# A hybrid S5 / RG-LRU / attention block: a fourth buffer of split weights, splits three units ahead, and the S5 tables as a task of their own

## The chip, the cores and the metric

The kernel runs on one core of one Trainium2 chip. The metric is device time in microseconds (us), the median of several runs. Engines are named as the profile names them: PE multiplies matrices (PEld is its weight load), ACT evaluates functions and copies, DVE does elementwise arithmetic, POOL is a second, slower elementwise engine, SP issues most DMAs.

## The reference

One layer, sequence 256, width 2048, everything in float32. Three branches run side by side on the same normed input, each is multiplied by a sigmoid gate, and a squared-ReLU MLP follows.

```python
xn = rms_norm(x)
u_s5, u_lru, q, k, v, gate_logits = split(xn @ w_in)       # 1024 x 5, then 3 x 2048
g_s5, g_lru, g_attn = split(sigmoid(gate_logits + b_gate))
# S5: 64 groups of 16 channels, 64 complex states each, diagonal linear scan over time
a = exp(lam * dt); h = linear_scan(a, B u); y = Re(C h) + d * u
y_s5 = gelu(y) * sigmoid(gelu(y) @ w_glu + b_glu)
# RG-LRU: causal conv of 4, two block-diagonal sigmoid gates, real linear scan
y_lru = linear_scan(exp(log_a), sqrt(1 - exp(2 log_a)) * (i * xc))
# stick-breaking attention, 8 heads of 128
w = exp(log_sigmoid(z) + reverse_cumsum(log_sigmoid(-z)))   # causal
merged = g_s5 * (y_s5 @ w_br_s5) + g_lru * (y_lru @ w_br_lru) + g_attn * (y_attn @ w_br_attn)
h = x + merged @ w_out
out = rms_norm(h + relu(rms_norm(h) @ w_up)**2 @ w_down)
```

## The kernel before

**Weights.** All weights pass once through the core as 520 units, each 256 rows by 512 columns of one matrix, 512 KB. The order is written in `stream`: w_in for the LRU (units 0 to 15) and for S5 (16 to 31); the LRU gate, four times eight units of w_in and four of w_br_lru (32 to 79); k, q, v twice (80 to 127); the attention gate, four times eight and four (128 to 175); two chunks of S5 gates (176 to 191); w_glu (192 to 199); the rest of the S5 gates with w_br_s5; w_out; w_up and w_down in turns.

**Splits.** A float32 product is done as three products of rounded parts. A unit is loaded by SP into a `raw` buffer (pool `wraw`, three buffers). `split_next` makes `hi`, the rounded copy, on ACT (line 146) and `lo = raw - hi` on DVE (line 147), in pool `whi`, three buffers of each. PE then does 12 matmuls of 512 columns for the unit (`chunk_tok`, lines 241 to 243; `pair_tok`, lines 276 to 278) or 24 of 256 columns (`chunk`, lines 225 to 227): hi by xhi, lo by xhi and hi by xlo. `next_unit(i)` issues loads up to unit i + 3 and splits up to unit i + 2 ahead of the products of unit i.

**Side tasks.** Everything else is written as Python generators. `later` puts one in a list with a rate; after the products of each unit `pump` steps each task by its rate, and what a step issues stands between the instructions of that unit. A scheduler then settles the order on each engine, and an engine executes its own instructions in that order.

**The S5 task.** `s5_scan` runs at rate `S5_RATE`, 1.27, from unit 32 on, over eight blocks of eight groups. For each block it needs a table of cosines and sines of the phases of its states over time (`tc`, `ts`, 128 x 1024). `s5_tables(b)` adds two small tables by broadcast (`fhi`, `flo`, two POOL products of 512 columns made once for all blocks), takes the fraction of a turn (line 606 on ACT, one DVE row), an Abs (line 609) and two Sin (lines 610 and 611). Its generator `more` is stepped by three `next(more, None)` inside the block before: the parts stand at fixed places of that block. A block multiplies by the table, scans over time, multiplies back and ends in the matmuls `ps_y`. After the last block come gelu (Square, Tanh) and `yg_hi`, `yg_lo`, the operands of w_glu.

**Gates and functions.** After a gate chunk the two banks are scaled and biased on DVE (line 750) and go through a Sigmoid on ACT (line 751). Sigmoid, Sin and the exponentials lie in different function tables, and ACT_TABLE_LOAD changes the table.

The functions that the change touches:

Of the kernel before, what the change touches and what calls it, by code (L numbers as in the profile page):

```python
# [14 lines left out]
P = 128  # L15
L = 256
# [30 lines left out]
def hybrid_block(ctx: ExitStack, tc: tile.TileContext, io, out):  # L47
# [61 lines left out]
    raw, hi, anchor = {}, {}, {}  # L109
    st = {"load": 0, "split": 0, "use": 0}  # L110

# [96 lines left out]
    def finish(task):  # L208
        while step(task):
            pass  # L210
# [21 lines left out]
    def chunk_tok(name, c, k, xs, hold=0, done=None):  # L232
# [77 lines left out]
    ux = sp.tile([P, 4, L], F32R, name="ux")  # L310
    stk = sp.tile([96, NT, 2, L], F32R, name="stk")
    rad = sp.tile([P, 32], F32, name="rad")
    fhi = sp.tile([P, 32, 16], F32, name="fhi")
    flo = sp.tile([P, 32, 16], F32, name="flo")
    pp = s5.enter_context(tc.tile_pool(name="s5w", bufs=1))
# [96 lines left out]
    def s5_params():  # L412
# [14 lines left out]
        g.tensor_scalar(b, b, math.pi, -math.pi, ALU.min, ALU.max)  # L427
        yield
        g.tensor_scalar(w, b, 1.0 / TWO_PI, None, ALU.mult)
# [3 lines left out]
        g.tensor_tensor(n, cr, n, ALU.subtract)  # L433
        sb = steps.unsqueeze(1).broadcast_to([P, 32, 16])
        g.tensor_tensor(flo, w.unsqueeze(2).broadcast_to([P, 32, 16]), sb, ALU.mult)
        g.tensor_tensor(fhi, n.unsqueeze(2).broadcast_to([P, 32, 16]), sb, ALU.mult)
        yield
# [56 lines left out]
    nc.gpsimd.memset(tiny, 2.0 ** -115)  # L494
    wr = lp.tile([P, WT, P], F32, name="wr")
    wi = lp.tile([P, WT, P], F32, name="wi")
    for t, src in ((wr, "lru_w_r"), (wi, "lru_w_i")):
# [97 lines left out]
    def s5_tables(b):  # L595
        c = pp.tile([P, NT, 16, 16], F32, tag="tc", name=f"tc{b}", bufs=2)
        s = pp.tile([P, NT, 16, 16], F32, tag="ts", name=f"ts{b}", bufs=2)
        q = slice(b * NT, (b + 1) * NT)
        sh = [P, NT, 16, 16]
        f = "p n a b -> p (n a b)"  # L600
        cf, sf = c.rearrange(f), s.rearrange(f)

        def gen():
            nc.vector.tensor_tensor(c, fhi[:, q, :].unsqueeze(3).broadcast_to(sh), flo[:, q, :].unsqueeze(2).broadcast_to(sh), ALU.add)
# [4 lines left out]
            nc.scalar.activation(cf, sf, AF.Abs)  # L609
            nc.scalar.activation(sf, sf, AF.Sin, scale=-TURN)  # L610
            nc.scalar.activation(cf, cf, AF.Sin, scale=-TURN, bias=half_pi)
            yield
        f = "p n a b -> p n (a b)"
        return (c.rearrange(f), s.rearrange(f)), gen()

    def s5_split(ct):
# [3 lines left out]
        for g in range(2):  # L620
            m = mask[:, g:g + 1]
            nc.scalar.activation(bx[0][:, :, g, :], bco[:, ct], AF.Copy, scale=m)
            nc.vector.scalar_tensor_tensor(bx[1][:, :, g, :], bco[:, ct], m, bx[0][:, :, g, :].bitcast(F32), ALU.mult, ALU.subtract)

    def s5_stack(t):
        for i, w_ in enumerate((ux[:, 0:4:2, :], ux[:, 1:3, :], ux[:, 0:4:3, :])):
            nc.sync.dma_start(stk[i * 32:i * 32 + 32, t].bitcast(F32), w_[t * 32:t * 32 + 32].bitcast(F32))
# [3 lines left out]
    def s5_scan():  # L631
# [11 lines left out]
        tt = nc.vector.tensor_tensor  # L643
        for b in range(WT):
            c, s = tabs
            t3 = pp.tile([P, NT, L], F32, tag="t3", name=f"t3_{b}")
            for t in range(NT):
# [22 lines left out]
            tt(t3, t3, vr, ALU.subtract)  # L670
            next(more, None)
            yield
            for x_ in (t1, t3):
                for t in range(NT):
# [4 lines left out]
                    yield  # L679
            next(more, None)  # L680
            tt(t2, t1, c, ALU.mult)
            yield
            tt(vr, t3, s, ALU.mult)
            next(more, None)
            yield
# [15 lines left out]
            if b % 2:  # L701
                gq.append(later([gelu(b)], 1.0))

    def tt_scan(o, r, i):
        nc.vector.tensor_tensor_scan(o, r, i, 0.0, ALU.mult, ALU.add)

    def gelu(b):
        y = us5[:, b - 1:b + 1, :]
        g1 = tmp.tile([P, 2, L], F32, tag="gate", name=f"g1_{b}", bufs=3)
        nc.scalar.activation(g1, y, AF.Square)  # L710
        nc.vector.scalar_tensor_tensor(g1, g1, 1.0 / GELU_K, y, ALU.add, ALU.mult)
        yield
        nc.scalar.activation(g1, g1, AF.Tanh, scale=GELU_C * GELU_K)
        nc.vector.scalar_tensor_tensor(y, g1, 1.0, y, ALU.add, ALU.mult)
        yield
# [19 lines left out]
    def gates(idx, c, alloc):  # L735
# [49 lines left out]
    def attention(hs, kT, qT, vt):  # L785
# [49 lines left out]
    for c in range(2):  # L835
# [10 lines left out]
        banks = chunk_tok("w_in", 8 + c, D, xs)  # L846
        vt = ap_.tile([P, 2, CH], F32, tag="v", name=f"vt{c}")
        for t in range(2):
# [73 lines left out]
    gp = small("norm_mlp_g")  # L922
    x_tok = mlp.tile([P, 2, D], F32, name="xres")

# [75 lines left out]
    gfb = mlp.tile([P, D], F32, name="gfb")  # L1000
    ho = mlp.tile([P, 2, D], F32, name="ho")
    ssq = mlp.tile([P, 2, 6], F32, name="ssq")
# [168 lines left out]
```

## Time and profile before

| | us |
|---|---|
| median of 3 runs | 1511.09 (1510.91 to 1512.21) |
| the profiled execution | 1512.1 |
| its span, first to last instruction | 1510.3 |
| PE busy | 1488.4 |
| DVE busy | 1175.2 |
| ACT busy | 782.3 |
| POOL busy | 35.3 |

The mean granted clock of PE is 0.995. In the rows of single engines the first number is the start from the beginning of the span, the second the duration, and what stands in brackets is the idle time before it with the work that ended it. Matmuls overlap, so a matmul's duration is longer than the distance to the next start, and a busy PE is not PE at its peak. In a table of stretches a value such as "7.82 (x51)" is busy time and count of instructions in that stretch.

### The profile page before, as it was taken

Reading aid. Unit: us, or ns where it says so; the run is one execution under the profiler, and the core shown is the slowest. Engines: PE = TensorE matmul, PEld = TensorE weight load, DVE = VectorE, ACT = ScalarE, POOL = GpSimd, SP = SyncE. Lnnn points to the kernel's source line nnn. Section 1 sums busy time; section 2 is a strip of 40 time slices with the busy share of each in tenths; the row PEclk is TensorE's granted clock in tenths of the full one; section 3 lists DMA queues with packets and bytes.
Section 4 is the critical chain, followed back from the end, with each engine's and each line's share of the span. In section 5 each row is a group of like instructions: output and inputs, shape, how many; then the busy total and the mean of one; then the engine's idle time right before and its main releaser. Section 6 shows DMA issues by size and latency. Waiting matters only on the chain.

```text
span 1510.3 us, 19900 instructions
## 1 busy us (share of the span) xinstructions
PE 1488.4 (99%) x7518; PEld 1260.5 (83%) x7518; DVE 1175.2 (78%) x1468; ACT 782.3 (52%) x920; POOL 35.3 (2%) x60
## 2 busy tenths in 40 slices
PE   9999999999999999999999999999999999999997
PEld 9997788989887878988887888888888888888886
DVE  6767998897988989689799796568854787558965
ACT  6767556565765564544455544344433444344443
POOL 1400000000000000000000000000000000000011
PEclk9999999999999999999999999999999999999999
DMA  9546766665555666666855666666666666666664
GB/s 287 157 153 176 228 205 201 187 182 168 175 172 183 208 182 210 189 202 190 276 182 188 197 184 205 194 185 196 198 194 193 193 195 195 195 191 191 192 197 152
DMA packets 89858, 292.41 MB, mean 194 GB/s; under 512 B 12834, under 2 KB 17058, under 8 KB 89634
## 3 DMA queue, kind: packets, MB, share of 16 engines
q1 hardware_dynamic: 89618, 291.07, 62.6%
q8 instruction: 59, 0.97, 0.3%
q14 instruction: 37, 0.30, 0.1%
q10 hardware_dynamic: 144, 0.07, 0.0%
HBM read 282.71 MB, written 2.10 MB: 189 GB/s over the span
## 4 chain that ended last, share of the span: by engine, by line
PE 83%; DVE 9%; issue 3%; ACT 2%; DMA 2%; SPq 0%; DVEq 0%; ACTq 0%
PE mt_w_up L242 6%; PE mt_w_up L241 6%; PE mt_w_up L243 6%; PE mt_w_in L242 5%; PE mt_w_in L243 5%; PE mt_w_in L241 5%; PE mt_w_down L242 4%; PE mt_w_down L241 4%; PE mt_w_down L243 4%; PE mp_w_down L277 4%; PE mp_w_down L278 4%; PE mp_w_down L276 4%; PE mm_w_in L227 4%; PE mm_w_in L225 4%; PE mm_w_in L226 4%; DVE lo L147 3%
## 5 line engine op out<-in xcount | busy, mean ns | idle before, releaser
L146 ACT CAST hi<-raw 128x1024 fp32r<-128x1024 f32 (+1 forms) x521 | 545.2, 1049 | 625.9 <-PE mt_w_up L243 131.4
L147 DVE TENSOR_TENSOR lo<-raw,hi 128x1024 fp32r<-128x1024 f32 (+1 forms) x521 | 637.9, 1225 | 287.7 <-ACT hi L146 284.1
L242 PE MATMUL mt_w_in<-lo,xhi 128*128 128x512 f32 x448 | 176.1, 393 | 3.9 <-DVE lo L147 3.7
L241 PE MATMUL mt_w_in<-hi,xhi 128*128 128x512 f32 x448 | 175.2, 396 | 0.2 <-ACT hi L146 0.2
L243 PE MATMUL mt_w_in<-hi,xlo 128*128 128x512 f32 x448 | 175.2, 391 | 0.0
L241 PE MATMUL mt_w_up<-hi,hhi 128*128 128x512 f32 x448 | 174.3, 389 | 0.0
L242 PE MATMUL mt_w_up<-lo,hhi 128*128 128x512 f32 x448 | 174.3, 389 | 0.0
L243 PE MATMUL mt_w_up<-hi,hlo 128*128 128x512 f32 x448 | 174.3, 389 | 0.0
L227 PE MATMUL mm_w_in<-xhi,lo 128*128 128x256 f32 x512 | 145.4, 286 | 4.5 <-DVE lo L147 4.5
L225 PE MATMUL mm_w_in<-xhi,hi 128*128 128x256 f32 x512 | 146.5, 286 | 0.5 <-ACT hi L146 0.4
L226 PE MATMUL mm_w_in<-xlo,hi 128*128 128x256 f32 x512 | 145.7, 285 | 0.0
L728 DVE STREAM_TRANSPOSE reluT<-relu 32x256 f32<-32x256 f32 x256 | 111.5, 436 | 4.2
L242 PEld LDWEIGHTS mt_w_in<-lo,xhi 128*128 128x128 f32 x448 | 84.6, 189 | 24.0 <-DVE lo L147 7.6
L227 PEld LDWEIGHTS mm_w_in<-xhi,lo 128*128 128x128 f32 x512 | 98.7, 194 | 5.5 <-DVE lo L147 5.5
L242 PE MATMUL mt_w_down<-lo,hd_hi 128*128 128x512 f32 (+1 forms) x272 | 102.5, 377 | 0.0
L241 PE MATMUL mt_w_down<-hi,hd_hi 128*128 128x512 f32 (+1 forms) x272 | 102.4, 377 | 0.0
L243 PE MATMUL mt_w_down<-hi,hd_lo 128*128 128x512 f32 (+1 forms) x272 | 102.4, 376 | 0.0
L225 PEld LDWEIGHTS mm_w_in<-xhi,hi 128*128 128x128 f32 x512 | 99.2, 194 | 1.1 <-ACT hi L146 1.0
L277 PE MATMUL mp_w_down<-lo,hd_hi 128*128 128x512 f32 x256 | 99.8, 390 | 0.1
L278 PE MATMUL mp_w_down<-hi,hd_lo 128*128 128x512 f32 x256 | 99.6, 389 | 0.0
L276 PE MATMUL mp_w_down<-hi,hd_hi 128*128 128x512 f32 x256 | 99.6, 389 | 0.0
L241 PEld LDWEIGHTS mt_w_in<-hi,xhi 128*128 128x128 f32 x448 | 84.5, 189 | 17.8 <-ACT hi L146 0.7
(299 smaller groups left out, 2370.2 us busy)
## 6 DMA issues: line engine op xcount, KB each, us to landing
raw<-in_w_in SPq DMA_DIRECT2D x175, 512.0 KB, 4.3
raw<-in_w_up SPq DMA_DIRECT2D x128, 512.0 KB, 4.2
raw<-in_w_down SPq DMA_DIRECT2D x128, 512.0 KB, 4.2
raw<-in_w_out SPq DMA_DIRECT2D x32, 512.0 KB, 4.2
raw<-in_w_br_lru SPq DMA_DIRECT2D x16, 512.0 KB, 4.6
raw<-in_w_br_attn SPq DMA_DIRECT2D x16, 512.0 KB, 4.1
raw<-in_w_br_s SPq DMA_DIRECT2D x16, 512.0 KB, 4.1
stk<-ux SPq DMA_DIRECT2D x96, 64.0 KB, 4.1
```

The lines of the kernel that those rows point to most:

```text
L146: anchor["act"] = nc.scalar.copy(h[:, k, :], r[:, k, :]).ins
L147: anchor["dve"] = nc.vector.tensor_tensor(l_[:, k, :], r[:, k, :], h[:, k, :].bitcast(F32), ALU.subtract).ins
L225: nc.tensor.matmul(o, wh[:, kk, s], xh, start=first and ct % 2 == 0, stop=False, skip_group_check=True)
L226: nc.tensor.matmul(o, wh[:, kk, s], xl, start=False, stop=False, skip_group_check=True)
L227: mm = nc.tensor.matmul(o, wl[:, kk, s], xh, start=False, stop=last and ct % 2 == 1, skip_group_check=True)
L241: nc.tensor.matmul(banks[j], xh[:, s], wh[:, a:b], start=kt == 0, stop=False)
L242: nc.tensor.matmul(banks[j], xh[:, s], wl[:, a:b], start=False, stop=False)
L243: return nc.tensor.matmul(banks[j], xl[:, s], wh[:, a:b], start=False, stop=kt == ng * UK - 1)
L276: nc.tensor.matmul(o, xh[:, s], wh[:, kk, :], start=kt == 0, stop=False)
L277: nc.tensor.matmul(o, xh[:, s], wl[:, kk, :], start=False, stop=False)
L278: mm = nc.tensor.matmul(o, xl[:, s], wh[:, kk, :], start=False, stop=kt == ng * UK - 1)
L728: nc.vector.transpose(d_[32 * a:32 * a + 32, :, :, 32 * b:32 * b + 32], s_[32 * b:32 * b + 32, :, :, 32 * a:32 * a + 32])
```

## The change

1. Pool `whi` gets a fourth buffer for hi and for lo, 8 KB a partition more. `next_unit(i)` issues loads up to i + 4 and splits up to i + 3. `wraw` keeps three buffers.
2. `fhi` and `flo` are no longer made for all blocks; `fw` keeps the phases of one step and of sixteen, and each block makes its own two small tables `ph` with two POOL products of 64 columns.
3. The tables of the next block are a task of their own, at the same rate, with three empty steps ahead and more empty steps inside. Its Sin pair is held while `st["chain"]` is set (an attention task is in its run of logits and exponentials) and while the last three units of a gate chunk are being issued. `finish(more)` at the next block issues what is left. The Tanh of gelu is held while `st["chain"]` is set.
4. Room for the buffers comes from shared tags: `stk` takes the place of the LRU matrices `wr`, `wi`; `vt` that of `kT`; `ho` that of `x_tok`.

```diff
-    whi = ctx.enter_context(tc.tile_pool(name="whi", bufs=3))
+    whi = ctx.enter_context(tc.tile_pool(name="whi", bufs=4))
...
-        while st["load"] <= min(i + 3, len(stream) - 1):
+        while st["load"] <= min(i + 4, len(stream) - 1):
...
-        while st["split"] <= min(i + 2, len(stream) - 1):
+        while st["split"] <= min(i + 3, len(stream) - 1):
...
+            st["left"] = ng - 1 - g          # in chunk_tok, after each unit
...
-        sb = steps.unsqueeze(1).broadcast_to([P, 32, 16])
-        g.tensor_tensor(flo, w.unsqueeze(2).broadcast_to([P, 32, 16]), sb, ALU.mult)
-        g.tensor_tensor(fhi, n.unsqueeze(2).broadcast_to([P, 32, 16]), sb, ALU.mult)
...
         def gen():                           # in s5_tables(b)
-            nc.vector.tensor_tensor(c, fhi[...], flo[...], ALU.add)
+            ph = pp.tile([P, 2, NT, 16], F32, tag="ph", name=f"ph{b}")
+            for k in range(2):
+                nc.gpsimd.tensor_tensor(ph[:, k], fw[:, k, q]..., steps..., ALU.mult)
+            yield
+            nc.vector.tensor_tensor(c, ph[:, 1]..., ph[:, 0]..., ALU.add)
+            yield
             yield
             nc.scalar.activation(sf, cf, AF.Identity, bias=magic)
             nc.vector.scalar_tensor_tensor(sf, sf, -MAGIC, cf, ALU.add, ALU.subtract)
             yield
+            yield
             nc.scalar.activation(cf, sf, AF.Abs)
+            yield
+            while st["chain"] or st["gate"] and st["left"] < 3:
+                yield
             nc.scalar.activation(sf, sf, AF.Sin, scale=-TURN)
             nc.scalar.activation(cf, cf, AF.Sin, scale=-TURN, bias=half_pi)
...
-            more = iter(())                  # in s5_scan, per block
             if b + 1 < WT:
                 s5_split(b + 1)
                 tabs, more = s5_tables(b + 1)
+                more = later([chain_of(3, more)], S5_RATE)
...
-            next(more, None)                 # three of these between the block's rows
...
+        while st["chain"]:                   # in gelu, ahead of the Tanh
+            yield
...
+        st["gate"] = True                    # in gates
         banks = chunk_tok("w_in", GATE0 + 4 * idx + c, D, xs)
+        st["gate"] = False
```

**ACT at the end of the second attention gate chunk** (units 144 to 151; `hi151` is the split of unit 151, `gate2_1_0` and `gate2_1_1` the two halves of the gate, `ts6` and `tc6` the tables of S5 block 6). Before:

```order
L146 CAST hi149_4625<-raw149_4603 128x1024
L606 ACTIVATE ts6_4381<-tc6_4380,magic_133 128x1024
L146 CAST hi150_4654<-raw150_4623 128x1024
L609 ACTIVATE tc6_4380<-ts6_4381 128x1024
L610 ACT_TABLE_LOAD
L610 ACTIVATE ts6_4381<-ts6_4381 128x1024
L751 ACT_TABLE_LOAD
L751 ACTIVATE gate2_1_0_4644<-gate2_1_0_4644 128x512
L751 ACTIVATE gate2_1_1_4647<-gate2_1_1_4647 128x512
L611 ACT_TABLE_LOAD
L611 ACTIVATE tc6_4380<-tc6_4380,half_pi_131 128x1024
L146 CAST hi151_4676<-raw151_4652 128x1024
```

After:

```order
L146 CAST hi151_4658<-raw151_4626 128x1024
L610 ACTIVATE ts6_4542<-tc6_4541,magic_131 128x1024
L770 ACTIVATE gate2_1_0_4648<-gate2_1_0_4648 128x512
L146 CAST hi152_4682<-raw152_4656 128x1024
L770 ACTIVATE gate2_1_1_4651<-gate2_1_1_4651 128x512
L146 CAST hi153_4704<-raw153_4680 128x1024
L614 ACTIVATE tc6_4541<-ts6_4542 128x1024
L618 ACT_TABLE_LOAD
L618 ACTIVATE ts6_4542<-ts6_4542 128x1024
L619 ACTIVATE tc6_4541<-tc6_4541,half_pi_129 128x1024
L146 CAST hi154_4730<-raw154_4702 128x1024
L146 CAST hi155_4756<-raw155_4728 128x1024
```

The run of rows between two CASTs held the Abs, three table loads, both Sin rows and both Sigmoids; now the Sigmoids stand between CASTs of 151 to 153, and the Abs, one table load and the Sin pair are the longest run.

**ACT at the start of S5** (`ylru_hi` is the operand of w_br_lru, `ux` the input of S5, `ts0` and `tc0` the first tables, `gate1_0` the first LRU gate). Before:

```order
L146 CAST hi37_1485<-raw37_1458 128x1024
L572 CAST ylru_hi_150<-lru_xc1_1069 128x512
L618 CAST ux_102<-us5_99 128x256
L622 ACTIVATE ux_102<-bco_100,par_79 128x2x64
L609 ACTIVATE tc0_1431<-ts0_1432 128x1024
L622 ACTIVATE ux_102<-bco_100,par_79 128x2x64
L610 ACT_TABLE_LOAD
L610 ACTIVATE ts0_1432<-ts0_1432 128x1024
L572 CAST ylru_hi_150<-lru_tc1_1073 128x512
L611 ACTIVATE tc0_1431<-tc0_1431,half_pi_131 128x1024
L146 CAST hi38_1510<-raw38_1483 128x1024
L146 CAST hi39_1531<-raw39_1508 128x1024
```

After:

```order
L146 CAST hi40_1525<-raw40_1504 128x1024
L614 ACTIVATE tc0_1433<-ts0_1434 128x1024
L146 CAST hi41_1543<-raw41_1523 128x1024
L146 CAST hi42_1561<-raw42_1541 128x1024
L146 CAST hi43_1587<-raw43_1559 128x1024
L770 ACT_TABLE_LOAD
L770 ACTIVATE gate1_0_0_1577<-gate1_0_0_1577 128x512
L770 ACTIVATE gate1_0_1_1580<-gate1_0_1_1580 128x512
L618 ACT_TABLE_LOAD
L618 ACTIVATE ts0_1434<-ts0_1434 128x1024
L619 ACTIVATE tc0_1433<-tc0_1433,half_pi_129 128x1024
L146 CAST hi44_1607<-raw44_1585 128x1024
```

Before, ten rows stood between the CASTs of 37 and 38. Now the CASTs of 38 to 43 stand between these rows (both `ylru_hi` and the `ts0` of line 610 already ahead of the fence), `ux` comes later, and the Sin pair stands behind the first gate's Sigmoids, ahead of the CAST of 44.

**DVE at the end of S5** (line 700 before and line 710 after adds the matmuls `ps_y7` to `us5`; line 750 before and 769 after scales the last S5 gate; lines 688 to 692 before and 698 to 702 after are the last products of a block). Before:

```order
L692 TENSOR_TENSOR s5_t_1430<-s5_t_1430,s5_v_1429 128x1024
L147 TENSOR_TENSOR lo191_5580<-raw191_5558,hi191_5579 128x1024
L147 TENSOR_TENSOR lo192_5598<-raw192_5577,hi192_5597 128x1024
L700 SCALAR_TENSOR_TENSOR us5_99<-us5_99,par_79,ps_y7_5613 128x256
L147 TENSOR_TENSOR lo193_5626<-raw193_5595,hi193_5625 128x1024
L711 SCALAR_TENSOR_TENSOR g1_7_5641<-g1_7_5641,us5_99 128x512
L750 SCALAR_TENSOR_TENSOR gate0_1_0_5644<-mt_w_in_11_0_184_5478,rstd_tok_136,gb0_1_5477 128x512
L750 SCALAR_TENSOR_TENSOR gate0_1_1_5647<-mt_w_in_11_1_184_5479,rstd_tok_136,gb0_1_5477 128x512
L714 SCALAR_TENSOR_TENSOR us5_99<-g1_7_5641,us5_99 128x512
L147 TENSOR_TENSOR lo194_5669<-raw194_5623,hi194_5668 128x1024
L875 SCALAR_TENSOR_TENSOR yg_lo_5653<-us5_99,yg_hi_5652 128x512
```

After:

```order
L696 TENSOR_TENSOR s5_t_1432<-s5_t_1432,s5_v_1431 128x1024
L700 TENSOR_TENSOR s5_t_1432<-s5_t_1432,ts7_4988 128x1024
L147 TENSOR_TENSOR lo195_5695<-raw195_5633,hi195_5694 128x1024
L702 TENSOR_TENSOR s5_t_1432<-s5_t_1432,s5_v_1431 128x1024
L147 TENSOR_TENSOR lo196_5725<-raw196_5692,hi196_5724 128x1024
L710 SCALAR_TENSOR_TENSOR us5_99<-us5_99,par_79,ps_y7_5663 128x256
L147 TENSOR_TENSOR lo197_5755<-raw197_5722,hi197_5754 128x1024
L726 SCALAR_TENSOR_TENSOR g1_7_5673<-g1_7_5673,us5_99 128x512
L147 TENSOR_TENSOR lo198_5785<-raw198_5752,hi198_5784 128x1024
L731 SCALAR_TENSOR_TENSOR us5_99<-g1_7_5673,us5_99 128x512
L147 TENSOR_TENSOR lo199_5829<-raw199_5782,hi199_5828 128x1024
L896 SCALAR_TENSOR_TENSOR yg_lo_5679<-us5_99,yg_hi_5678 128x512
```

The last S5 products stood ahead of the gate's rows and now stand behind them; the gelu rows stand between the splits of 196 to 199.

**PE at the same place** (`ps_y7` are the last S5 matmuls, `mt_w_in_11` the last S5 gate chunk, `mm_w_glu_0` and `mm_w_glu_1` the two w_glu chunks). Before:

```order
L242 MATMUL mt_w_in_11_1_184_5479<-lo190_5561,xhi_82 128x512
L243 MATMUL mt_w_in_11_1_184_5479<-hi190_5560,xlo_83 128x512
L698 MATMUL ps_y7_5613<-s5_t_1430,ce_101 32x256 x8
L241 MATMUL mt_w_in_11_0_184_5478<-hi191_5579,xhi_82 128x512
L242 MATMUL mt_w_in_11_0_184_5478<-lo191_5580,xhi_82 128x512
```

After, two pieces, the second further down where `mm_w_glu_0` takes up its last unit:

```order
L225 MATMUL mm_w_glu_0_0_192_5690<-yg_hi_5678,hi193_5616 128x256
L226 MATMUL mm_w_glu_0_0_192_5690<-yg_lo_5679,hi193_5616 128x256
L708 MATMUL ps_y7_5663<-s5_t_1432,ce_101 32x256 x4
L227 MATMUL mm_w_glu_0_0_192_5690<-yg_hi_5678,lo193_5617 128x256
L225 MATMUL mm_w_glu_0_0_192_5690<-yg_hi_5678,hi193_5616 128x256
```

```order
L225 MATMUL mm_w_glu_1_0_196_5824<-yg_hi_5678,hi197_5754 128x256
L226 MATMUL mm_w_glu_1_0_196_5824<-yg_lo_5679,hi197_5754 128x256
L225 MATMUL mm_w_glu_0_0_192_5690<-yg_hi_5678,hi195_5694 128x256
L225 MATMUL mm_w_glu_0_1_192_5691<-yg_hi_5678,hi195_5694 128x256
L227 MATMUL mm_w_glu_1_0_196_5824<-yg_hi_5678,lo197_5755 128x256
```

`ps_y7` moved from inside the last gate chunk, ahead of w_glu, into the first w_glu chunk in two halves, and matmuls of the second w_glu chunk now stand ahead of the first one's last unit.

More of the change, by code (lines that the diff above doesn't have):

```diff
@@ L109, in hybrid_block @@
     raw, hi, anchor = {}, {}, {}
-    st = {"load": 0, "split": 0, "use": 0}
+    st = {"load": 0, "split": 0, "use": 0, "gate": False, "left": 0, "chain": False}
     def pieces(i):
@@ L310, in hybrid_block @@
     ux = sp.tile([P, 4, L], F32R, name="ux")
-    stk = sp.tile([96, NT, 2, L], F32R, name="stk")
     rad = sp.tile([P, 32], F32, name="rad")
-    fhi = sp.tile([P, 32, 16], F32, name="fhi")
-    flo = sp.tile([P, 32, 16], F32, name="flo")
+    fw = sp.tile([P, 2, 32], F32, name="fw")
     pp = s5.enter_context(tc.tile_pool(name="s5w", bufs=1))
@@ L494, in hybrid_block @@
     nc.gpsimd.memset(tiny, 2.0 ** -115)
-    wr = lp.tile([P, WT, P], F32, name="wr")
-    wi = lp.tile([P, WT, P], F32, name="wi")
+    wrwi = sp.tile([P, 2, WT, P], F32, tag="stk", name="wrwi")
+    wr, wi = wrwi[:, 0], wrwi[:, 1]
     for t, src in ((wr, "lru_w_r"), (wi, "lru_w_i")):
@@ L623, in s5_split @@
             nc.vector.scalar_tensor_tensor(bx[1][:, :, g, :], bco[:, ct], m, bx[0][:, :, g, :].bitcast(F32), ALU.mult, ALU.subtract)
+    stk = sp.tile([P, NT, 2, L], F32R, tag="stk", name="stk")[0:96]
     def s5_stack(t):
@@ L636, in s5_scan @@
         yield from more
+        more = None
         s5_split(0)
@@ L644, in s5_scan @@
         for b in range(WT):
+            if more is not None:
+                finish(more)
             c, s = tabs
@@ L683, in s5_scan @@
             tt(vr, t3, s, ALU.mult)
-            next(more, None)
             yield
@@ L702, in s5_scan, with chain_of @@
                 gq.append(later([gelu(b)], 1.0))
+    def chain_of(n, gen):
+        for _ in range(n):
+            yield
+        yield from gen
     def tt_scan(o, r, i):
@@ L922, in hybrid_block @@
     gp = small("norm_mlp_g")
-    x_tok = mlp.tile([P, 2, D], F32, name="xres")
+    x_tok = mlp.tile([P, 2, D], F32, tag="rows", name="xres")
     def x_load():
@@ L1000, in hybrid_block @@
     gfb = mlp.tile([P, D], F32, name="gfb")
-    ho = mlp.tile([P, 2, D], F32, name="ho")
+    ho = mlp.tile([P, 2, D], F32, tag="rows", name="ho")
     ssq = mlp.tile([P, 2, 6], F32, name="ssq")
```

14 lines of the change are left out of this document (10 added, 4 removed).

## Prediction

> **What bounds the kernel now.** I read the page first, then the table of stretches, the list of waits, and the rows of single engines around the longest waits.
>
> ```profile
> span 1510.3 us, 19900 instructions
> ...
> PE 1488.4 (99%) x7518; PEld 1260.5 (83%) x7518; DVE 1175.2 (78%) x1468; ACT 782.3 (52%) x920; POOL 35.3 (2%) x60
> ...
> L146 ACT CAST hi<-raw 128x1024 fp32r<-128x1024 f32 (+1 forms) x521 | 545.2, 1049 | 625.9 <-PE mt_w_up L243 131.4
> L147 DVE TENSOR_TENSOR lo<-raw,hi 128x1024 fp32r<-128x1024 f32 (+1 forms) x521 | 637.9, 1225 | 287.7 <-ACT hi L146 284.1
> ...
> raw<-in_w_in SPq DMA_DIRECT2D x175, 512.0 KB, 4.3
> ```
>
> PE is nearly always busy, and the split of a weight unit costs 1.05 us of ACT and 1.23 us of DVE. The change does not touch the matmuls, so it can win only where PE stands still or runs slowly. The profiled execution took 1512.1 us (span 1510.3), 1.0 above the median; the sum goes against 1512.1 and I take one microsecond off at the end.
>
> I looked for stretches in which PE is not full (columns: length, busy time and count of PE, PEld, DVE, ACT, POOL, granted clock). I took thirteen around PE's waits for splits from 40 us on; six of them and the sum of the thirteen:
>
> ```profile
> 46.00:54.00 8.00, 6.24 (x50) 5.83 (x49) 7.96 (x15) 7.45 (x13) 5.40 (x10) 1.00 0.39 108
> 86.00:96.00 10.00, 7.82 (x51) 7.42 (x50) 10.00 (x18) 4.43 (x6) 0.00 (x0) 0.83 0.44 120
> 114.00:134.00 20.00, 17.08 (x67) 13.01 (x66) 18.07 (x25) 17.14 (x22) 0.00 (x0) 0.91 0.48 142
> 150.00:192.00 42.00, 41.35 (x179) 32.94 (x178) 40.53 (x45) 23.88 (x27) 0.00 (x0) 1.00 0.70 215
> 480.00:490.00 10.00, 7.63 (x26) 5.58 (x25) 5.94 (x6) 6.24 (x8) 0.00 (x0) 0.83 0.46 147
> 804.00:812.00 8.00, 7.06 (x31) 5.18 (x30) 7.99 (x12) 5.63 (x8) 0.00 (x0) 1.00 0.52 173
> sum 124.00, PE 112.44 PEld 88.60 DVE 113.94 ACT 76.35 POOL 5.40; mean PE 8.65 PEld 6.82 DVE 8.76 ACT 5.87 POOL 0.42
> ```
>
> Idle there: 124.00 - 112.44 = 11.6 us. The clock lost 0.17 x 10 + 0.09 x 20 + 0.17 x 10 = 5.2 us. Who ended PE's waits (total, times, longest; the three largest of the eleven rows in which a split ends them, 26 waits and 22 us together):
>
> ```profile
> PEld mt_w_in L242 <- DVE lo L147: 7.6, 9, 2.3
> PEld mm_w_in L227 <- DVE lo L147: 5.5, 5, 2.1
> ...
> PEld mt_w_br_attn L241 <- ACT hi L146: 2.6, 1, 2.6
> ```
>
> PE waits for hi or lo of a unit, that is, for a split that came late. One such wait, PE alone:
>
> ```profile
> 129.18 0.50 PE L242 MATMUL mt_w_in<-lo,xhi 128*128 128x512 f32 x1 [1.91 <-DVE lo L147]
> 129.51 0.39 PE L243 MATMUL mt_w_in<-hi,xlo 128*128 128x512 f32 x1
> 129.74 0.39 PE L242 MATMUL mt_w_in<-lo,xhi 128*128 128x512 f32 x1
> ...
> 130.32 0.63 PE L241 MATMUL mt_w_in<-hi,xhi 128*128 128x512 f32 x1
> 130.74 0.63 PE L242 MATMUL mt_w_in<-lo,xhi 128*128 128x512 f32 x1
> ```
>
> Matmuls start 0.23 apart, but the last one ahead of a wait counts as 0.39 busy and the first after it takes 0.33 to the next start: (0.39 - 0.23) + (0.33 - 0.23) = 0.26 us a wait that the idle column hides, 26 x 0.26 = 7 us. And from 130.32 on starts are 0.42 apart, half speed: the 5.2 us above are after-effects of waits. In all 11.6 + 5.2 + 7 = 24 us hang on late splits. That is the most this change can give.
>
> [...]
>
> **Why a split comes late.** ACT at the worst gate end:
>
> ```profile
> 473.81 1.06 ACT L146 CAST hi<-raw 128x1024 fp32r<-128x1024 f32 x1 [0.49 <-PE mt_w_in L243]
> 474.77 1.05 ACT L609 ACTIVATE tc<-ts 128x1024 f32<-128x1024 f32 x1
> 475.84 1.28 ACT L610 ACT_TABLE_LOAD   x1
> 477.13 1.06 ACT L610 ACTIVATE ts<-ts 128x1024 f32<-128x1024 f32 x1
> 478.20 1.28 ACT L751 ACT_TABLE_LOAD   x1
> 479.50 1.15 ACT L751 ACTIVATE gate<-gate 128x512 f32<-128x512 f32 x2
> 480.65 1.28 ACT L611 ACT_TABLE_LOAD   x1
> 481.95 1.15 ACT L611 ACTIVATE tc<-tc,half_pi 128x1024 f32<-128x1024 f32 x1
> 483.00 2.92 ACT L146 CAST hi<-raw 128x1024 fp32r<-128x1024 f32 x3
> ```
>
> Between two CASTs ACT is away from 474.77 to 483.00, 8.2 us. A unit lasts 12 x 0.227 = 2.72 us on PE. With splits two ahead, the CAST at 473.81 (released by the end of a unit) leaves ACT 3 x 2.72 = 8.2 us until PE needs the next; with 1.05 for the earlier CAST and 1.05 for its own it comes 2.1 us late, the 2.2 to 2.6 us that PE waits. Three ahead, the time is 4 x 2.72 = 10.9 us.
>
> **The change, part by part.**
> *Fourth hi/lo buffer, one split further.* Each cluster gets 2.72 us more. What it does not lift is throughput: raw still has three buffers, and a load waits for the split three before it. A raw buffer turns in 4.3 + 1.05 + 1.23 = 6.6 us, 2.2 us a unit, under 2.72; with one 1.2 us product ahead of lo on DVE it is 7.8 / 3 = 2.6. So the lead can fill where DVE has room, slowly (0.1 to 0.5 us a unit), and not where DVE is full: 10.00 of 10.00 at 86 to 96, 40.53 of 42 at 150 to 192.
> *Tables as a task with holds.* At that gate end the order now has CASTs of 152 and 153 between the two gate sigmoids and the Sin pair, and the longest run without a CAST is L614, load, two Sin = 1.05 + 1.28 + 1.06 + 1.15 = 4.5 us. At the first S5 block, the run of 7.3 us (ylru_hi, ux, Abs, table, Sin pair) falls apart into single rows with a CAST behind each; a run gate pair + two loads + Sin pair of 1.15 + 2.56 + 2.21 = 5.9 us is left ahead of the CAST of 44. With a CAST of 1.05 before and one behind it and lo 1.23 that is 9.2 us, under 10.9: no wait. The longest run, with three loads at the last attention gate, is 1.15 + 3.84 + 2.21 = 7.2, with the CASTs and lo 10.5, also under 10.9 but by 0.4 only.
> *Two table loads fewer* (33 to 31): 2.6 us of ACT, covered by an engine that is 52% busy; nothing.
> *Two POOL products of 512 columns become sixteen of 64.* What they do to DVE, from the two old ones:
>
> ```profile
> 43.66 0.43 DVE L348 SCALAR_TENSOR_TENSOR rs<-ps_n,rs 128x256 f32<-128x256 f32 x1
> 44.12 1.01 DVE L349 SCALAR_TENSOR_TENSOR rstd<-rs,rs 128x256 f32<-128x256 f32 x1
> ...
> 45.65 0.25 POOL L445 TENSOR_TENSOR prm<-prm 128x32 f32<-128x32 f32 x1
> 45.86 1.06 POOL L436 TENSOR_TENSOR fhi<-prm,par 128x512 f32<-128x512 f32 x1
> ```
>
> Beside such a product a DVE row of 0.43 took 1.01. One of 64 columns lies between 0.25 (32) and 1.06 (512), nearest 0.3; it can hold DVE that long: 16 x 0.3 = 4.8 us at most, if every one hit where DVE is the bound. DVE is 78% busy and only the first two blocks lie in a full stretch: 4 x 0.3 = 1.2 at most, I take 0.5. [...]
> *Shared tags* (stk with wr/wi, v with k, x_tok with ho): each is a wait for an earlier reader. stk is first written after the products with wr and wi; v is written at the end of its chunk, whose first units issue the logits that read k, and the next k eight units after that attention's end; ho comes after x_tok's last reader. I take 0 for these. But attention's DVE work now stands against a lo burst of six units from 127 on; six lo are 7.3 us, six units 16.3, so it costs 0 to 1 by what attention puts between: 0.5.
> *S5 runs later.* The tables wait, so the last ps_y moves from ahead of the end of the S5 gates into w_glu chunk 0, and PE fills with chunk 1 before it uses yg. Durations from S5's end before:
>
> ```profile
> 601.36 0.48 DVE L700 SCALAR_TENSOR_TENSOR us<-us,par,ps_y 128x256 f32<-128x256 f32 x1 [1.44 <-PE ps_y L698]
> 602.89 0.69 DVE L711 SCALAR_TENSOR_TENSOR g<-g,us 128x512 f32<-128x512 f32 x1
> 603.62 1.44 DVE L750 SCALAR_TENSOR_TENSOR gate<-mt_w_in,rstd_tok,gb 128x512 f32<-128x512 f32 x2
> ...
> 601.88 0.63 ACT L710 ACTIVATE g<-us 128x512 f32<-128x512 f32 x1 [0.50 <-DVE us L700]
> 606.36 0.61 ACT L874 ACTIVATE yg_hi<-us 128x512 fp32r<-128x512 f32 x1
> ...
> 609.99 1.05 ACT L146 CAST hi<-raw 128x1024 fp32r<-128x1024 f32 x1 [1.83 <-PE mm_w_glu L226]
> 612.83 1.05 ACT L146 CAST hi<-raw 128x1024 fp32r<-128x1024 f32 x1 [1.79 <-PE mm_w_glu L226]
> ```
>
> A w_glu unit is 24 matmuls in 2.84 us, 0.12 each. From T, the end of the gate chunk: a product's tail 1.1, gate pair 1.4, four rows of 1.2 on DVE: 7.3; ps_y reaches PE after 62 w_glu matmuls and four of its own, T + 7.9, and ends at 8.3. Then us 0.5, Square 0.6, lo 1.2, g 0.7, Tanh 0.6, us 0.7, CAST 1.05, yg_hi 0.6: T + 14.2. PE comes to it after 72 + 38 matmuls of w_glu and 8 of ps_y: 118 x 0.12 = T + 14.2. A tie; between 0 and 3 (a lo and a CAST more in the way) I take 1.0.
>
> **The sum.** Of the 24 us, left standing: 0.8 at 46 to 54 (ACT 7.45 of 8 busy with the norm), 0.5 each at 86 to 96, 114 to 134 and 150 to 192 (DVE full), and 2 in scattered waits that I cannot place. New: 1.0 at S5's end, 0.5 attention, 0.5 POOL. 24 - 4.3 - 2.0 = 17.7, against the profiled run 1494; less one for the median, 1493.
>
> **Rivals.**
> *The lead does not fill* (three raw buffers, full DVE). Then 86 to 96, 150 to 192, 804 to 812 and 46 to 54 keep their waits, and the gate and table ends win: 480 to 490 (2.4 + 1.7 + 0.5) and 114 to 134 (2.9 + 1.8 + 0.8), about 10, less 2 new: 1503. For it: DVE at 10.00 of 10.00. Against: these stretches are 10 to 20 us long with roomy ones ahead of them, and one unit banked is 2.72 us against waits of at most 2.1. 17%.
> *All of it comes back*, nothing new: 1511 - 24 = 1487. 15%.
> [...] 5%.
> *Slower: tables too late.* The Sin pair is held through gate ends and attention; if it comes after the next block's first product is due, DVE stands in its order before `t1 = vr * c`, and all later lo with it. Price a block: a wait as at 129 (2.2) with its half clock (1.8), 4.0. It decides from five blocks of seven (20 > 17.7); at six, 1493 + 24 = 1517. Against: in the order eight units, 22 us, lie between a block's last Sin and the first product that reads it (the CAST of 43 and lo of 51 in the first block). 7%.
> *It does nothing* (the order holds splits where they were): 1511. Against: the CAST of 153 stands now ahead of the Sin pair. 5%.
>
> **How the numbers follow.** My case, 1488 to 1499, holds 51%. A measurement here tells 0.2%, 3 us, from no change. Faster: 51 + 17 + 15 + 5 = 88%, less 2 for what small costs add up to, 86; same 5 + 1 = 6; slower 7 + 1 = 8. The range: all-back less 2 at the bottom, 1485, the unfilled lead at the top, 1503; outside lie the slower and the idle case and a part of the ends.
>
> **What would show it.** At gate ends CASTs between sigmoids and Sin, PE idle in the thirteen stretches under 4 us, granted clock 1.00 where 0.83 and 0.91 stand; the list of waits with splits under 5 us in all; yg near 0 to 3 us in w_glu. Wrong would make it: waits of PE for lo that remain in full-DVE stretches, or rows of S5's first product that end a wait of DVE for the Sin pair.

## The result, and the profile after

The changed kernel took 1500.53 us (median of 5, 1498.47 to 1502.66) against 1511.26 of the kernel before; the ratio is 0.9926, 95% interval 0.9912 to 0.9941. It is 10.7 us faster, where 18 were forecast. The profiled execution took 1501.15 us, against 1512.1 before: 11.0 less.

From the page after:

```profile
span 1499.4 us, 19910 instructions
...
PE 1479.6 (99%) x7518; PEld 1256.1 (84%) x7518; DVE 1172.7 (78%) x1468; ACT 777.8 (52%) x918; POOL 56.5 (4%) x74
...
L146 ACT CAST hi<-raw 128x1024 fp32r<-128x1024 f32 (+1 forms) x521 | 545.3, 1050 | 624.4 <-PE mt_w_up L243 117.0
L147 DVE TENSOR_TENSOR lo<-raw,hi 128x1024 fp32r<-128x1024 f32 (+1 forms) x521 | 636.6, 1223 | 280.1 <-ACT hi L146 276.0
```

The work is the same but for POOL, which goes from 35.3 to 56.5 us. The stretches that answer to those of before, shifted a little since everything now comes earlier, and three more near the end of S5 (length, busy time of PE, PEld, DVE, ACT, POOL, clock, share and rate of the DMA):

```profile
46.00:54.00 8.00, 7.99 (x67) 7.78 (x66) 7.96 (x16) 7.78 (x14) 4.26 (x10) 1.00 0.33 101
84.00:94.00 10.00, 9.23 (x75) 8.97 (x74) 10.00 (x19) 4.04 (x7) 0.00 (x0) 1.00 0.37 122
110.00:132.00 22.00, 22.00 (x98) 18.22 (x98) 19.18 (x24) 14.85 (x17) 2.98 (x2) 1.00 0.65 198
148.00:190.00 42.00, 40.16 (x177) 31.89 (x176) 33.30 (x37) 24.83 (x29) 0.55 (x2) 1.00 0.76 224
470.00:490.00 20.00, 20.00 (x90) 16.57 (x89) 19.72 (x23) 12.08 (x12) 0.00 (x0) 1.00 0.67 221
540.00:548.00 8.00, 5.85 (x25) 4.28 (x25) 4.38 (x4) 7.04 (x9) 0.00 (x0) 1.00 0.31 113
556.00:562.00 6.00, 5.08 (x29) 3.33 (x28) 4.81 (x7) 2.90 (x6) 0.00 (x0) 1.00 0.67 225
596.00:612.00 16.00, 13.90 (x118) 12.48 (x117) 11.95 (x13) 6.78 (x9) 0.00 (x0) 1.00 0.54 165
```

The start of S5 (110 to 132) and the gate end (470 to 490), where PE had been idle for 2.9 and 2.4 us, are full, and their granted clock is 1.00 instead of 0.91 and 0.83. But 148 to 190 has lost more than before (1.8 against 0.7 us), and 5.2 us are now missing in three stretches after 540; the kernel before had been idle for 0.1 us in all of 500 to 650. Who ends PE's waits:

```profile
PEld ps_y L708 <- issue: 3.2, 7, 1.1
...
PEld mt_w_in L242 <- DVE lo L147: 2.8, 4, 1.1
PEld mt_w_in L241 <- ACT hi L146: 2.2, 2, 1.8
PEld ps_v L663 <- ACT s_v L665: 2.2, 2, 1.4
PEld mm_w_in L227 <- DVE lo L147: 1.9, 4, 1.0
PEld ps_v L663 <- DMA stk<-ux: 1.5, 1, 1.5
PEld mm_w_in L225 <- ACT hi L146: 1.5, 1, 1.5
PEld mm_w_glu L225 <- ACT yg_hi L895: 1.4, 1, 1.4
PEld ps_y L708 <- DVE s_t L702: 1.3, 2, 0.9
```

Two things are seen. Waits of PE for splits fell from 26 with 22 us to 12 with 9 us. And there are new names: the matmuls of S5 itself, ps_v, ps_y and yg_hi in w_glu, 6.4 us. At one ps_y of lead_only PE stood idle for 2.03 us until the operand was there, and the weight matmuls behind it in PE's order started after it (last section).

Worked out over all PE intervals, the time by which starts lie further apart than 0.227 us (512 columns) or 0.12 us (256) fell by 11 us in all. By stretches: 100 to 150 won 6.3, 450 to 500 won 5.4, 0 to 100 won 4.6, 700 to 950 won 3.0; 150 to 300 lost 2.2 and 500 to 650 lost 6.5; from 300 to 450 nothing moved by more than 0.3.

### The profile page after: what moved, and what is told of

Read it like the earlier page. It is cut to its first block, busy times and chain, and to the rows that moved or that the text cites. A ratio compares the mean times of both kernels' runs of the same rounds, so it can differ in the third digit from the quotient of the medians.

```text
span 1499.4 us, 19910 instructions
## 1 busy us (share of the span) xinstructions
PE 1479.6 (99%) x7518; PEld 1256.1 (84%) x7518; DVE 1172.7 (78%) x1468; ACT 777.8 (52%) x918; POOL 56.5 (4%) x74
## 4 chain that ended last, share of the span: by engine, by line
PE 77%; DVE 11%; DMA 5%; ACT 4%; issue 3%; SPq 0%; DVEq 0%; ACTq 0%
PE mt_w_up L241 7%; PE mt_w_up L243 7%; PE mt_w_up L242 7%; DVE lo L147 4%; PE mp_w_down L278 4%; PE mp_w_down L279 4%; PE mp_w_down L277 4%; PE mt_w_down L242 4%; PE mt_w_down L241 4%; PE mt_w_down L243 4%; PE mt_w_in L243 3%; PE mt_w_in L241 3%; PE mt_w_in L242 3%; DMA raw<-in_w_in 3%; PE mm_w_in L227 2%
```

## The experiments

Theory A: the longer lead of splits makes the gain, and the table task gives some of it back. Theory B: the tables' new places make the gain. First the halves of the change apart.

**lead_only.** The buffers, the lead and the tags stay; the tables are stepped as before. The task's empty steps and the hold of the Tanh go too (not in the cut below); the POOL products for each block stay, issued as soon as the block before asks for its tables.

```diff
-                more = later([chain_of(3, more)], S5_RATE)
+            next(more, None)        # at the three places of the kernel before
-            while st["chain"] or st["gate"] and st["left"] < 3:
-                yield
```

> Fourth hi/lo buffer, loads four and splits three ahead, and the shared tags stay; the S5 tables are stepped at three fixed places inside the block before, without holds, as in the kernel before (the two small tables come from POOL per block). Theory A (the gain comes from the longer lead; the table task pays for itself only at gate ends and gives the rest back because S5 runs later and PE stands at ps_v, ps_y and yg_hi): S5's own waits, 6 us in the list, and the stall near 543 go, some gate ends with the tables in them come back with 1 to 3 us each at lead 2: 1496 to 1500, at or below the changed kernel's 1500.5. Theory B (the gain comes from the tables' new places, the longer lead stands mostly empty behind three raw buffers): 1505 or more.

**tables_only.** The other half:

```diff
-    whi = ctx.enter_context(tc.tile_pool(name="whi", bufs=4))
+    whi = ctx.enter_context(tc.tile_pool(name="whi", bufs=3))
-        while st["load"] <= min(i + 4, len(stream) - 1):
+        while st["load"] <= min(i + 3, len(stream) - 1):
-        while st["split"] <= min(i + 3, len(stream) - 1):
+        while st["split"] <= min(i + 2, len(stream) - 1):
```

> Splits two and loads three ahead with three hi/lo buffers as before; the S5 tables are a task with holds as in the changed kernel. Theory A: gate end at 480 to 490 and start of S5 win 6 to 8 us, the later S5 end costs 7 or more: 1508 to 1515. Theory B: most of the gain is here, 1500 to 1504.

Measured: lead_only 1497.64 us (1497.32 to 1498.87), ratio 0.9911 [0.9898, 0.9925]; tables_only 1510.13 (1507.93 to 1511.50), 0.9991 [0.9982, 1.0]. The lead alone wins at least what the whole change wins, the tables alone win nothing that can be told. B falls, and since tables_only also has the shared tags and the POOL products for each block, these don't make the gain either. The medians put the cost of the table task on top of the lead at 2.9 us; the spreads of the two kernels just touch (1497.32 to 1498.87 against 1498.47 to 1502.66). lead_only also has PE standing at S5's own matmuls:

```profile
PEld ps_y L703 <- DVE s_t L697: 2.6, 2, 2.5
...
PEld ps_v L655 <- DVE us L705: 1.4, 1, 1.4
...
PEld ps_v L655 <- DMA stk<-ux: 0.7, 1, 0.7
```

so these waits come with either form of the tables; the table task adds to them and moves them to S5's end: by the distances between starts lead_only loses 1.5 us between 500 and 650 and the changed kernel 7.4, of which 2.7 are the waits for splits at 543.

**no_holds.**

```diff
-            while st["chain"] or st["gate"] and st["left"] < 3:
-                yield
-        while st["chain"]:           # ahead of gelu's Tanh
-            yield
```

> The changed kernel without the three holds (Sin pair at gate ends and in attention, Tanh in attention); the task and its empty steps stay. Theory A: Sin pairs come at the task's own pace, some fall on gate ends, which a lead of 2 to 2.5 covers there, and S5 ends one to four units earlier: 1498 to 1502. Theory B: the holds make the gain, and it goes back by 4 us or more: 1504 to 1508.

Measured: 1500.16 (1499.06 to 1500.83), 0.9926 [0.9912, 0.9939]: the changed kernel's time. The holds don't make the gain, and in sum they cost nothing that can be told. That sum may hide two parts: without them PE waits 3.4 us for a hi at a gate end at 180, which the changed kernel does not, and the mean granted clock of the profiled execution is 0.998 against 0.999; and the wait for yg_hi is gone from the list. The run of 1499.06 to 1500.83 lies clear above lead_only, so the task costs something without its holds as well.

**start_early.** Since S5 ends late, let it start earlier:

```diff
-            yield
-            while st["chain"] or st["gate"] and st["left"] < 3:
+            if b:
+                yield
+            while b and (st["chain"] or st["gate"] and st["left"] < 3):
                 yield
```

> The changed kernel, but the tables of block 0 alone are made without the hold (and without one empty step), so that S5 starts earlier. Theory A: PE's waits near 597 and 609 (1.05 and 1.4 us) and a part of that near 543 (3 us) go: 1495 to 1499. Rival: the start's cluster returns to 120 to 134 (up to 3 us) and the S5 end's waits stay since the rate, not the start, sets the end: 1500 to 1504.

Measured: 1504.77 (1502.05 to 1507.10), 0.9956 [0.9942, 0.9969]. My expectation failed, and the time lies a little over the rival's range too; the profiled execution, 1507.1, is the slowest of the five. All later blocks moved too, and one Sin pair now meets a gate end with a lead of less than one unit. ACT there:

```profile
170.23 1.05 ACT L146 CAST hi<-raw 128x1024 fp32r<-128x1024 f32 x1 [1.24 <-DMA raw<-in_w_br_lru]
171.30 1.28 ACT L619 ACT_TABLE_LOAD   x1
172.59 1.06 ACT L619 ACTIVATE ts<-ts 128x1024 f32<-128x1024 f32 x1
173.67 1.28 ACT L771 ACT_TABLE_LOAD   x1
174.97 1.15 ACT L771 ACTIVATE gate<-gate 128x512 f32<-128x512 f32 x2
176.14 1.28 ACT L620 ACT_TABLE_LOAD   x1
177.43 1.15 ACT L620 ACTIVATE tc<-tc,half_pi 128x1024 f32<-128x1024 f32 x1
178.49 2.92 ACT L146 CAST hi<-raw 128x1024 fp32r<-128x1024 f32 x3
```

It is the run of 7.2 us that I had priced at nothing with a full lead (10.5 under 10.9). PE waited 2.79 us for the CAST at 178.49. A second wait of this size, 2.88 us of idle, stands at 550 at a ps_y that waits for a row of S5 on DVE. Behind the first, matmuls of 512 columns start 0.43 us apart instead of 0.23; the mean granted clock of the execution is 0.995, against 0.999 in the changed kernel's. By the distances between starts, 500 to 650 did win 2 us against the changed kernel, but 150 to 300 lost 4 and 450 to 500 lost 3. The CAST ahead of the run had waited for a DMA; with three units in hand it could have been done long before. So the question became why the lead is not full.

**lead_psy_late.** Before that, the S5 matmuls' place in PE's order, on lead_only:

```diff
+            yield
+            yield
             ps = pss.tile([P, CH], F32, tag="ps", name=f"ps_y{b}")
...
-    S5_RATE = 1.27
+    S5_RATE = 1.38
```

> lead_only with two more empty steps ahead of each block's ps_y, and a rate of 1.38 instead of 1.27 so that S5 ends at about the same unit. If the waits of PE at S5's own matmuls (4.7 us for s_t, us and stk in lead_only) come from where these stand in PE's order, they go, with the half clock behind the longest: 1493 to 1496. Rival: the higher rate puts more of S5's rows per unit on DVE, lo comes later, and the waits only change their name: 1497 to 1501.

Measured: 1499.31 (1498.98 to 1500.23), 0.9918 [0.9903, 0.9933], 1.7 above lead_only: the rival. The waits at ps_y are gone from the list, but lo came later (10 waits for lo of 6.8 us against 6 of 3.4), and ps_v waited 2.1 for us. Moving S5's matmuls in PE's order did not pay: what they wait for are S5's rows on DVE. The rate was raised in the same run, so how much of the later lo comes from it is not told apart.

**raw4 and raw3_cut.** The load of a unit waits until the split three before it has read its raw buffer. In the changed kernel the rows of the list in which a CAST waits for a raw DMA add up to 212 us in 137 waits (138 us in 84 before the change); the largest is

```profile
ACT hi L146 <- DMA raw<-in_w_in: 92.5, 59, 4.1
```

The lead, counted from the trace as units whose lo has ended less units whose matmuls PE has begun (a unit half begun counts as half), had a mean of 0.66 between 150 and 200 and 1.3 to 1.5 between 500 and 600, where the program allows three units beyond the one in hand. The lead does fill elsewhere: between 300 and 500 the same count gives 2.4, and 1.3 in the kernel before; between 150 and 200 the kernel before has 0.8 and lead_only 1.2, so there nothing of the fourth hi/lo buffer is left in the changed kernel. So a fourth raw buffer; its 4 KB come from attention's `s` and the gate tiles, and a control has those cuts alone.

```diff
-    wraw = ctx.enter_context(tc.tile_pool(name="wraw", bufs=3))
+    wraw = ctx.enter_context(tc.tile_pool(name="wraw", bufs=4))   # raw4 only
...
-            s_ = ap_.tile([P, Z], F32, tag="s", name=f"s{h}", bufs=3)
+            s_ = ap_.tile([P, Z], F32, tag="s", name=f"s{h}", bufs=2)
...                                          # tag "gate" in pool tmp: bufs=3 to bufs=2
```

> The changed kernel with a fourth raw buffer; room for it comes from two instead of three buffers of attention's s and of the gate tiles. Ring theory (three raw buffers keep the lead of splits near one unit where DVE is full, since a load waits for a lo that waits in DVE's order): mean lead at 150 to 200 and 500 to 600 rises by 0.5 units or more, PE's waits for hi and lo fall from 9 us to 4 or less, and it is 4 to 8 us below raw3_cut. Rival (DVE's and ACT's order alone sets it): within 2 us of raw3_cut.

> Control for raw4: the changed kernel with two instead of three buffers of attention's s and of the gate tiles, three raw buffers as before. Both theories: 1500 to 1504, as the changed kernel or a little over it, from gate tiles that wait for their readers.

Measured: raw3_cut 1499.81 (1498.53 to 1501.14), 0.9921 [0.9906, 0.9935]; raw4 1491.68 (1491.24 to 1492.33), 0.9867 [0.9852, 0.9882], 8.1 us below its control, a little over the 4 to 8 that I expected. In raw4 the largest waits of CASTs for a DMA are:

```profile
ACT hi L146 <- DMA raw<-in_w_in: 19.6, 13, 6.9
ACT hi L146 <- DMA raw<-in_w_up: 7.4, 4, 1.9
ACT hi L146 <- DMA raw<-in_w_br_lru: 6.4, 5, 2.2
```

and the stretches in which the changed kernel lost:

```profile
84.00:94.00 10.00, 10.00 (x81) 9.82 (x79) 10.00 (x19) 4.60 (x7) 0.00 (x0) 1.00 0.48 142
148.00:190.00 42.00, 41.44 (x186) 33.93 (x185) 36.24 (x40) 27.78 (x32) 0.55 (x2) 1.00 0.79 242
500.00:550.00 50.00, 49.22 (x230) 39.64 (x229) 47.46 (x54) 28.54 (x32) 0.00 (x0) 1.00 0.65 197
550.00:600.00 50.00, 49.77 (x286) 42.70 (x285) 45.51 (x49) 24.09 (x27) 0.00 (x0) 1.00 0.64 198
600.00:650.00 50.00, 50.00 (x258) 42.92 (x257) 38.94 (x50) 25.82 (x33) 0.00 (x0) 1.00 0.63 196
```

The waits of CASTs for raw fell to 35 us in 24; the four waits of PE for hi or lo that are left add up to 3.0 us. Between 500 and 650 PE is idle for 1.0 us, against 5.2 in the changed kernel, and between 550 and 600 the lead is 2.3 units instead of 1.5. It stays near 1 between 150 and 200 (1.04 against 0.62 in the control) and hardly rises between 500 and 550 (1.58 against 1.54): my 0.5 everywhere was too simple, and even so the waits went.

From 147 to 152, just ahead of where the lead is lowest, something else than the ring holds the loads. All loads stand in one queue, SP's, and S5 puts its own transfers `stk<-ux` into it. In the changed kernel:

```profile
142.59 4.52 SPq L637 DMA_DIRECT2D stk<-ux  x5
147.21 0.53 SPq L130 DMA_DIRECT2D raw<-in_w_in  x1
147.78 1.87 SPq L637 DMA_DIRECT2D stk<-ux  x3
149.75 0.53 SPq L130 DMA_DIRECT2D raw<-in_w_in  x1
```

Over the whole trace a load is issued 0.03 us (the median) after the lo three units before it has ended, which is the ring at work. The two loads shown at 147.21 and 149.75 and the next went 3.7, 5.1 and 3.1 us after it, behind the transfers, and the CAST at 152.04 waited 4.1 us for its raw. A fourth buffer does not change that queue: in raw4 loads between 100 and 150 went up to 6.5 us late. Of the 1.8 us that PE is idle between 148 and 190, 1.1 are ps_v's wait for one of these transfers, at 153. No run moves them, so what they cost in all is not shown.

**lead_raw4.** The same with the old stepping of the tables.

> lead_only with a fourth raw buffer and the same two cuts as raw4. Ring theory: waits for splits and the S5 waits behind them both fall, 1490 to 1495. Rival: 1497 to 1501, as lead_only with the cuts.

Measured: 1494.37 (1493.51 to 1495.36), 0.9883 [0.9866, 0.9899], 3.3 below lead_only and 2.7 above raw4. With the splits three ahead the table task wins with four raw buffers and loses with three.

**raw4_lead2_tables and raw4_lead2_old.** Is the fourth hi/lo buffer then needed? Four raw buffers and loads four ahead, but three hi/lo buffers and splits two ahead, without the cuts; with the table task, and with the old stepping.

```diff
-    whi = ctx.enter_context(tc.tile_pool(name="whi", bufs=4))
+    whi = ctx.enter_context(tc.tile_pool(name="whi", bufs=3))
-        while st["split"] <= min(i + 3, len(stream) - 1):
+        while st["split"] <= min(i + 2, len(stream) - 1):
```

> Four raw buffers and loads four ahead, but three hi/lo buffers and splits two ahead; the table task as in the changed kernel (no other cuts). Theory A with the ring (a lead is needed at both ends: raw that has landed, and a free hi/lo to split into): gate ends and full-DVE stretches keep their waits since the split still waits for a hi/lo buffer, 1501 to 1508. Rival (the ring alone is the bottleneck, the fourth hi/lo buffer does nothing with four raw buffers): 1491 to 1496.

> The same with the S5 tables stepped inside the blocks as in the kernel before: against the kernel before, the fourth raw buffer (and loads one further) alone. Theory A with the ring: gate ends keep their 4 us each, waits of CASTs for raw go, 1504 to 1510. Rival: 1493 to 1498.

Measured: 1501.47 (1501.31 to 1501.80), 0.9933 [0.9919, 0.9947], and 1503.16 (1502.59 to 1503.56), 0.9943 [0.9930, 0.9955]; the second is a little less than I expected. In raw4_lead2_old no wait of a CAST for a DMA stands in the first 40 rows of ACT's waits, but the gate end that the prediction showed waits as before:

```profile
PEld mt_w_br_attn L241 <- ACT hi L146: 2.6, 1, 2.6
```

All eight corners, medians in us (the last column has the cuts, which by the control change the time by -0.7, less than the spread of a kernel's runs; all corners but the kernel before also have the shared tags and the POOL products for each block):

| tables | 3 raw, splits 2 ahead | 3 raw, splits 3 ahead | 4 raw, splits 2 ahead | 4 raw, splits 3 ahead |
|---|---|---|---|---|
| in the block, as before | 1511.3 (the kernel before) | 1497.6 | 1503.2 | 1494.4 |
| a task of their own | 1510.1 | 1500.5 (the change) | 1501.5 | 1491.7 |

Each buffer wins alone, in the first row 8.1 us (raw) and 13.7 (hi/lo), and the two together 16.9: the rival that the fourth hi/lo buffer does nothing beside four raw buffers falls, and the gains add up only in part.

## Why the prediction was right or wrong

The time lay in the range and the direction held; the predicted gain of 18 was 10.7. It lay outside my case, 1488 to 1499, and the range held it because its top was drawn from a rival. Of the 7 us between forecast and result 5.5 lie between 500 and 650, where I had priced 1.0 and 6.5 were lost. Of the signs that I named, the clock and the wait for yg came, and the CASTs between Sigmoids and Sin at the second attention gate but not at the last; the waits for splits, 9.0 us, are not under 5, and PE's idle time in the thirteen stretches, 4.8 us, is not under 4; and a sign of being wrong came, a wait for lo in a full-DVE stretch (84 to 94, DVE 10.00 of 10.00).

*What hangs on late splits, 24 us.* Right in its parts: the gate end and the start of S5 are full, the scattered waits after 700 are gone, and so are the dips of the clock. raw4 wins 19.6 to 20 us (1511.26 or 1511.69 less 1491.68), near the sum that I drew from the waits.

*The clock.* Right: with the waits at 129 and 484 the half speed went (1.00 at 110 to 132 and at 470 to 490), 0.995 became 0.999. That the dips do not belong to the waits, to which I gave 5%, fell.

*The lead fills "where DVE has room, slowly".* This step failed. I bounded the ring of three raw buffers at 2.2 us a unit, 2.6 with one product ahead of lo, and concluded that it keeps up with 2.72. The runs show a CAST waiting for raw 137 times, and that one more raw buffer is worth 8.1 us. Two S5 or gate rows ahead of a lo make it 9.0 / 3 = 3.0, over 2.72, and then the lead runs down: between 500 and 600, 11 of 32 units have their lo start 2.3 us or more after their CAST has ended. Between 150 and 200 it is 3 of 18, and there the loads behind the `stk` transfers, which the working leaves out, come on top. Where DVE has room the step was right (2.4 units between 300 and 500). I had this as a rival with 1503 and 17%, and spoke against it with stretches "10 to 20 us long with roomy ones ahead"; but S5's rows stand between the lo of units all through S5, and 1500.5 is nearer to that rival than to my case. That nearness is in part luck: two of the stretches that it had keep their waits, 46 to 54 and 804 to 812, are full (the second in the changed kernel's trace at 8.00 of 8.00), and the loss lies mostly after 500, where it had 1.0.

*The run of 7.2 us at the last attention gate, no wait "by 0.4".* Failed for the same cause: it was priced with a lead of three that was not there. PE in the changed kernel:

```profile
541.87 0.39 PE L243 MATMUL mt_w_br_attn<-hi,ya_lo 128*128 128x512 f32 x1
543.64 0.49 PE L241 MATMUL mt_w_in<-hi,xhi 128*128 128x512 f32 x1 [1.38 <-ACT hi L146]
544.90 0.50 PE L242 MATMUL mt_w_in<-lo,xhi 128*128 128x512 f32 x1 [0.77 <-DVE lo L147]
```

2.2 us idle and 2.7 by start-to-start distance.

*S5 runs later: 1.0 us at yg.* The place was right and the size near:

```profile
609.16 0.50 PE L225 MATMUL mm_w_glu<-yg_hi,hi 128*128 128x256 f32 x2 [1.21 <-ACT yg_hi L895]
```

But I priced only this one of S5's meetings with PE. ps_v and ps_y, 5 us in the list, were in no term and in no rival: I had asked what is late for PE among the weights, and not what else stands in PE's queue that will be late next.

*Attention: 0.5.* Not seen: unit 127 begins at 410 in the kernel before, and 300 to 450 has moved by no more than 0.3 us. *Sixteen POOL products: 0.5.* The right size: DVE's rows beside them are longer by 0.7 us in all (last section), though each product is not 0.3 us long but 1.0 in the median. *Tables too late for the next block*: no wait of that kind appeared. *Shared tags*: one wait names one, ps_v's 1.5 us for `stk`; it ended with a transfer of the queue shown above, not with a reader of `wr` or `wi`. They were not tried apart.

What stays open: why the table task's sign turns with the raw buffers. The table of corners shows that it does; that S5's late end meets a low lead and so cannot be caught up fits the stretches from 500 to 650, and is not shown by a run that moves S5's end alone (start_early, meant to be that, moved everything). What the `stk` transfers in the queue of the loads cost stays open too.

## What to carry to other kernels

A prefetch through several rings of buffers can gain from each of them: here each ring deepened alone won (8.1 and 13.7 us), and both together won more (16.9). Before deepening one, count for each buffer of the chain how long it is held, with the consumer's worst queue ahead, compare with the pace, and look at what else stands in the queue of the loads. Read the lead that is actually there (what is finished less what is begun) before pricing a stall by the lead the program allows. And when one kind of wait is taken away from an engine, list what else stands in its order with an operand from a late engine; here that was the next wait (S5's own matmuls, 6.4 us).

## What the runs showed of the hardware

Half clock came behind waits of about 2 us again, but not behind all of them. In lead_only it stands behind 2.03 us of idle at a ps_y; in tables_only 1.93 us of idle ended at 91.94, and the clock stayed full (columns as above):

```profile
186.35:189.76 3.41, 1.38 (x12) 0.62 (x11) 3.41 (x5) 0.95 (x1) 0.00 (x0) 1.00 0.68 220
189.76:193.17 3.41, 3.41 (x11) 2.87 (x11) 1.53 (x2) 1.96 (x4) 0.00 (x0) 0.50 0.80 223
...
88.23:91.64 3.41, 1.79 (x15) 1.58 (x14) 3.41 (x7) 1.84 (x3) 0.00 (x0) 1.00 0.34 132
91.64:95.05 3.41, 3.10 (x26) 3.11 (x27) 3.41 (x8) 0.00 (x0) 0.00 (x0) 1.00 0.62 167
```

In the kernel before, each half-clock stretch in mid-kernel lasts 3.41 us and begins a whole number of 3.41 us after the clock first rose: 25, 36 and 140 of them after 7.19 us, at 92.5, 130.1 and 485.1. Counted in windows of this length from 7.19 us on, PE is idle there for 1.93, 1.90 and 2.37 us in the three windows just ahead of the half clock, and for 1.32 us at most in any other up to 1500. In the changed kernel, counted likewise from its own first rise at 4.16 us, no window up to 1490 has more than 1.29 us of idle, and the clock stays full. Its two waits at 543, 1.38 and 0.77 us, fall on both sides of a border of two such windows (1.20 and 0.94 us of idle); in raw3_cut two of 0.81 and 0.77 at the same place lie in one window, 1.58 together, and had half clock behind them (mean granted clock of that execution 0.997, against 0.999). In tables_only the window from 88.23 to 91.64 had 1.62 us of idle and none behind it, so the idle time of a window, counted in this way, does not part the cases sharply, and why the clock falls is not shown.

Where products of POOL and rows of DVE ran side by side here, it was POOL's that grew most. The 16 products of 64 columns took 0.29 us four times and 0.67 to 4.0 twelve times:

```profile
L604 POOL TENSOR_TENSOR ph<-fw,par x16: 292/974/4015, 45.1 to 464.4; 128x64 f32<-128x64 f32 x16
```

while the rows of DVE that ran beside one of the two longest pairs, 225.94 to 230.58, kept their duration (1.22 for a product or a lo, as in the median over the trace) until a product of POOL ended, where a row is 0.02 to 0.10 us longer than its like:

```profile
225.78 1.22 DVE L147 TENSOR_TENSOR lo<-raw,hi 128x1024 fp32r<-128x1024 f32 x1
226.92 1.22 DVE L683 TENSOR_TENSOR t<-t,s_v 128x1024 f32<-128x1024 f32 x1
228.05 1.22 DVE L147 TENSOR_TENSOR lo<-raw,hi 128x1024 fp32r<-128x1024 f32 x1
```

The prediction had read the opposite from one row, a DVE instruction that took 1.01 beside a POOL product of 512 columns. The 0.43 that it set against it is another instruction's; the same one (`rstd<-rs,rs`) takes 0.52 in the changed kernel, beside a product of 64 columns that took 0.29. So beside a long product of POOL this row of DVE was 0.5 us longer, and beside the sixteen short ones the rows of DVE were 0.7 us longer together.
